# A trunk with dilated attention on one core: the odd layer in two phases, with block products for its projections

## The chip, the core and the metric

The kernel runs on one core of one Trainium2 chip. The metric is the device time of one execution in microseconds; runs are summed up by their median. TensorE (PE) multiplies matrices, with its weight loads shown apart (PEld), VectorE (DVE) and ScalarE (ACT) do element-wise work and empty PSUM, GpSimd (POOL) does element-wise work in SBUF, and SyncE (SP) issues most DMAs. Each engine works through its own instructions in order.

## What is computed

Two decoder layers on x (1024 tokens, 1024 channels), each a mixer and a gated ConvFFN, with normalisation, shift, scale and gate ahead of each. The even layer mixes by a gated delta rule and window pooling; the odd layer, which the change is about, by dilated attention in three groups, eight heads of 128 each:

```
DIL_PATTERNS = ((128, 1), (512, 4), (2048, 16))       # window, dilation
for gi, (window, dil) in enumerate(DIL_PATTERNS):
    cols = w_in[:, gi * 3 * ATT_W:(gi + 1) * 3 * ATT_W]          # 1024 x 3072
    proj = (h @ cols).reshape(B, T, 3, ATT_HEADS, ATT_DH)
    q = rms_norm(proj[:, :, 0], q_norm) * (ATT_DH ** -0.5)
    k = rms_norm(proj[:, :, 1], k_norm)
    v = proj[:, :, 2]
    o, lse = dilated_band_attention(q, k, v, dil, window // dil, slopes)
    outs.append(o); lses.append(lse)
wts = jax.nn.softmax(jnp.stack(lses), axis=0)
o = jnp.sum(wts[..., None] * jnp.stack(outs), axis=0)
return o.reshape(B, T, ATT_W) @ w_out                             # 1024 x 1024
```

The mixer's result, times a gate, is added to x; the second ConvFFN follows.

## The kernel before

Every fp32 product is three matmuls on parts: `split` (L178) rounds an operand to `hi` on ACT (L179) and subtracts it to `lo` (L180) on an engine given to it; hi·hi, hi·lo and lo·hi are summed in PSUM. Weights come as granules of 128 x 512 (`granule`, L182: a DMA on SP's queue, then a split with the engine in `lo_eng`). h, the normalised x, lies transposed in eight tiles of 128 channels x 1024 tokens, as `hh` and `hl`. There are two wide PSUM slots (`mm`, 1024 columns) and four of 512 (`sp`). `big` tiles (24) and `t2k` tiles (8) are rings of SBUF buffers.

The first FFN's up-projection (`up`, L1224) already uses seven block products: h and the weight are cut into 2 x 2 blocks, sums of blocks are formed on DVE (L1164 for h, L1219 for weights), seven products of half the size take the place of eight, and DVE adds them together (L1236).

In `odd` the projection of 9216 columns is 18 sections of 512 columns: six of v (two for each group) and twelve of queries and keys (one for each group and pair of heads, `todo`). A section is four calls of `tproj`, one for 256 tokens, of 8 k-tiles x 2 x 3 matmuls 128x512 (L1344 to L1346). A v section is copied by ACT (L1438), stored to DRAM by POOL's queue (L1441) and loaded again, gathered by the dilation (L1412). Queries and keys are normalised over each head (`qk_norm`: squares on ACT L1355, reduce on DVE L1356, `rsqrt` in small DVE operations L119 to L127, product L1362), transposed on PE (`qk_turn`, L1376) and copied to the SBUF tiles `qkT`, still in SBUF when attention reads them.

`attend` takes a pair of heads of a group in eight units (256 tokens of one head): scores (L1496), bias (DVE L1508), maximum (L1512 or L1516), its negative (L1519), exponential with its sum (ACT L1521), transposes (L1529), copy (DVE L1531 or ACT), values (L1540), copy (ACT L1542) and a DMA to DRAM (`osc`) for every group. `merge` loads the three groups' results for 128 tokens and a pair of heads, weighs them (ACT L1591, DVE L1593) and transposes the result (`turn_o`, L1599).

The order: `weave` runs a chain (here `chains`, attention and merges) and between its steps takes from `dense` (projections, then output projection) at least as much PE time as the step's `need` names: 1.7, 2.0, 1.3 or 2.4 us. Attention of a pair runs beside the projections of the next two pairs. The output projection (`update`, L216; `wide=True` uses an `mm` slot and L239) takes rows 0 to 3 while attention still runs; the four last row blocks are the edge (`edge_start`, L402), which also starts the next norm. x is stored to DRAM at the layer's start (`spill`, L1286) and loaded again for the output projection. `lo_eng` is DVE in this layer (L1287).

Of the kernel before, what the change touches and what calls it, by code (L numbers as in the profile page):

```python
# [17 lines left out]
P = 128  # L18
# [7 lines left out]
HA = 8  # L26
# [8 lines left out]
def trunk(ctx, tc, x, c, ada_w, ada_b, norm_mix, norm_ffn, ev_w_in, ev_w_out, gdn_conv_w,  # L35
# [35 lines left out]
    def t2k():  # L71
        return tmp("t2k", [P, HALF], 8)
# [1008 lines left out]
    def ffn(l, xt, h, vec, acc, vec_next):  # L1081
        gate = mod[l][:, 40:48]
        wu, wd = ffn_w_up[l], ffn_w_down[l]
        with tc.tile_pool(name=f"pf{l}", bufs=1) as pf:
# [193 lines left out]
            acc = edge(*last, v, h2)  # L1278
            return xt, h2, v, acc


    def odd(xt, h, vec, acc):
# [3 lines left out]
        spill(xs[1], xt)  # L1286
        lo_eng[0] = nc.vector  # L1287
        with tc.tile_pool(name="po", bufs=1) as po:
            def et(tag, bufs, shape=(P, HALF), dt=F32):
                return tmp(tag, shape, bufs, dt, pl=po)  # L1290
# [33 lines left out]
            def section(g, kind, i):  # L1324

                base, out_ = g * 3072, []
                for k in range(KT):
                    rows = w[k * P:(k + 1) * P, :]
                    if kind == "v":
                        out_.append(granule(rows[:, base + 2048 + i * HALF:base + 2048 + (i + 1) * HALF]))  # L1330
                    else:
                        out_.append(granule(rows[:, base:base + 2048].rearrange("p (s c) -> p s c", s=2)
                                            [:, :, i * 256:(i + 1) * 256], ("p (s c) -> p s c", dict(s=2))))
                return out_

            def tproj(wg, b2):

                ps = mm_ps()
                for k in range(KT):
                    for i in range(2):  # L1340
                        hh, hl = (t[:, (b2 * 2 + i) * P:(b2 * 2 + i + 1) * P] for t in h[k])
                        wh, wl = wg[k]
                        p = ps[:, HS[i]]
                        nc.tensor.matmul(p, hh, wh, start=(k == 0), stop=False)  # L1344
                        nc.tensor.matmul(p, hh, wl, start=False, stop=False)  # L1345
                        nc.tensor.matmul(p, hl, wh, start=False, stop=(k == KT - 1))  # L1346
                        yield 3 * MM
                return ps

            def qk_norm(ps):  # L1350

                r, rr, ra = (et(t, 2, (P, 8)) for t in ("r", "rr", "ra"))
                for i in range(2):
                    sq = t2k()
                    nc.scalar.activation(sq, ps[:, HS[i]], AF.Square)  # L1355
                    nc.vector.tensor_reduce(out=r[:, i * 4:(i + 1) * 4], in_=sq.rearrange("p (a d) -> p a d", d=P),  # L1356
                                            axis=mybir.AxisListType.X, op=ALU.add)
                rsqrt(rr, r, 1.0 / P, ra)
                qk = []
                for i in range(2):  # L1360
                    qk.append(t2k())
                    nc.vector.tensor_tensor(out=qk[i].rearrange("p (a d) -> p a d", d=P),  # L1362
                                            in0=ps[:, HS[i]].rearrange("p (a d) -> p a d", d=P),
                                            in1=rr[:, i * 4:(i + 1) * 4, None].to_broadcast([P, 4, P]), op=ALU.mult)
                return qk

            def qk_turn(i, b2, qk):

                g = todo[i][0]
                if b2 == 0:  # L1370
                    qks[i] = [et("qkT", 4, (P, 2, T)) for _ in range(2)]
                for s in range(2):
                    ps = s_ps()
                    for hh in range(2):
                        for j in range(2):
                            nc.tensor.transpose(ps[:, (hh * 2 + j) * P:(hh * 2 + j + 1) * P],  # L1376
                                                blk4(qk[j])[s * 2 + hh], ident)
                    if g == 0:
                        dst = qks[i][s][:, :, b2 * 256:(b2 + 1) * 256]
                        src = ps.rearrange("p (h f) -> p h f", h=2)  # L1380
                    else:
                        r = 4 * g
                        n = 256 // r
                        dst = qks[i][s].rearrange("p h (r l) -> p h r l", r=r)[:, :, :, b2 * n:(b2 + 1) * n]
                        src = ps.rearrange("p (h l r) -> p h r l", h=2, r=r)
                    if s == 0:
                        nc.scalar.activation(dst, src, AF.Copy, scale=gq)
                    else:
                        nc.vector.tensor_copy(dst, src)
                ready.add((i, b2))  # L1390

            todo = [(g, hp) for hq in range(2) for g in (1, 2, 0) for hp in (2 * hq, 2 * hq + 1)]
            vd = {}
            turn = []

            def run_turn(at):
                turn[0][0] -= at
                if turn[0][0] <= 0:
                    qk_turn(*turn.pop(0)[1:])

            def load_values(i):

                g, hp = todo[i]
                d = vd[(g, hp // 2)][:, hp % 2 * 256:(hp % 2 + 1) * 256]
# [12 lines left out]
            def dense():  # L1417
                for i, (g, hp) in enumerate(todo):
                    while i >= 2 and ("att", i - 2) not in ready:
                        yield None  # L1420
                    hq = hp // 2
                    if (g, hq) not in vd:
                        wg = section(g, "v", hq)
                        for b2 in range(4):
                            gen = tproj(wg, b2)
                            if i == 0 and b2 == 0:
                                weave(norm(xt, vec, h, 1, acc, (1.8, 4.5)), gen)
                            while True:
                                try:
                                    c = next(gen)  # L1430
                                except StopIteration as e:
                                    ps = e.value
                                    break
                                if turn:
                                    run_turn(1)
                                yield c
                            v = big(F32, "v")
                            nc.scalar.copy(v, ps)  # L1438
                            if b2 == 0:
                                vd[(g, hq)] = dram.tile([T, HALF], F32, name=f"vd{g}{hq}")  # L1440
                            nc.gpsimd.dma_start(vd[(g, hq)][b2 * 256:(b2 + 1) * 256].rearrange("(i p) c -> p i c", p=P),  # L1441
                                                v.rearrange("p (i c) -> p i c", i=2))
                    load_values(i)
                    wg = section(g, "qk", hp)
                    for b2 in range(4):
                        gen = tproj(wg, b2)
                        while True:
                            try:
                                c = next(gen)
                            except StopIteration as e:  # L1450
                                ps = e.value
                                break
                            if turn:
                                run_turn(1)
                            yield c
                        turn.append([10, i, b2, qk_norm(ps)])
                lo_eng[0] = nc.gpsimd
# [3 lines left out]
                for ks in ((0, 1), (2, 3)):  # L1461
                    upd = update(row_blocks(od_w_out[0], ks), o, gate, res["x"], BY_TILE, wide=True)
                    for n, c in enumerate(upd):
                        if turn:
                            run_turn(1)
                        if n == 4 and ks[0] == 0:
                            o = [from_dram(osp2[i]) for i in (2, 3)]
                        yield c
# [7 lines left out]
            def attend(i, need):  # L1476
                g, hp = todo[i]
                dil = DILS[g]
                vs = vss[i]
                vb = lambda blk, hh: vs[blk // 4][:, blk % 4 * 256 + hh * P:blk % 4 * 256 + (hh + 1) * P]  # L1480
                un = [(b2, hh) for b2 in range(4) for hh in range(2)]
                stg, sbs, spans, pTs = {}, {}, {}, {}

                def scores(n):
                    b2, hh = un[n]
                    if hh == 0:
                        stg[b2] = et("stg", 2, (P, 2, 2, 130))
# [234 lines left out]
```

## Time and profile before

| | |
|---|---|
| three runs | 3086.98, 3090.63, 3090.97 us; median 3090.63 |
| the profiled execution | 3091.38 us, of which the span (first to last instruction) 3089.7 |
| mean granted TensorE clock | 0.987 |
| odd layer: first projection matmul, first edge matmul | 1267.7 us, 2345.6 us from the span's start |
| idle PE from 1380 to 2270 us | 6.0 of 890 us |
| busy DVE and POOL from 1380 to 2270 us | 466.8 and 40.1 us |

The profile's rows name line, engine and operation, the output tile, an arrow and the inputs, then shapes, the count, busy time, and the mean of one in ns; behind the last bar stands the engine's idle time ahead of them and what ended it. In a timeline a row is start, duration, engine, and what the engine waited for. Matmuls overlap, so that their spacing, not their duration, is what one costs.

### The profile page before, as it was taken

The page shows a single profiled execution, that of the slowest core. Times are in us where ns is not written, and L with a number is a line of the kernel's source. Part 1 is how long each engine was busy: PE and PEld are TensorE (multiplying, and loading weights), DVE is VectorE, ACT ScalarE, POOL GpSimd, SP SyncE. Part 2 cuts the span into 40 slices and gives each one's busy share as a digit, 9 for nine tenths or more (in the row PEclk, how much of TensorE's full clock was granted, in tenths as well). Part 3 has the DMA queues.
Part 4 walks back from the last instruction along what each step waited for, and adds up shares of the span by engine and source line. Part 5 has one row for each costly group of instructions (what it writes and reads, how often), then busy time and mean ns, then how long its engine had stood idle before and what let it go on. Part 6 is the DMA issues. An engine that isn't in the chain of part 4 may idle for free.

```text
span 3089.7 us, 40200 instructions
## 1 busy us (share of the span) xinstructions
PE 2975.0 (96%) x14346; PEld 2444.9 (79%) x14346; DVE 2018.4 (65%) x3877; ACT 1074.4 (35%) x2170; POOL 974.9 (32%) x727
## 2 busy tenths in 40 slices
PE   6999999899999899999999999999999899999999
PEld 4777777678888777788888878888877788888888
DVE  7768745987777787754454646354687876666554
ACT  4434422433333211323333433324343433333220
POOL 4412323565555543100000010000022655555540
PEclk8999999999999999999999999999999999999999
DMA  7523323243322754231313242313243222224321
GB/s 249 143 59 102 95 83 129 72 150 109 109 86 92 248 164 123 96 96 61 106 57 113 63 154 68 115 39 118 68 164 112 85 89 82 82 82 163 113 89 59
DMA packets 275010, 331.46 MB, mean 107 GB/s; under 512 B 27411, under 2 KB 194426, under 8 KB 274810
## 3 DMA queue, kind: packets, MB, share of 16 engines
q1 hardware_dynamic: 266810, 300.55, 30.8%
q0 software_dynamic: 7040, 25.17, 2.4%
q10 hardware_dynamic: 960, 3.18, 0.3%
q8 instruction: 113, 1.85, 0.2%
q14 instruction: 87, 0.71, 0.1%
HBM read 251.82 MB, written 77.00 MB: 106 GB/s over the span
## 4 chain that ended last, share of the span: by engine, by line
PE 72%; DVE 8%; DMA 2%; issue 2%; POOL 1%; ACT 1%; SPq 0%; POOLq 0%; DVEq 0%; ACTq 0%
PE sp L202 11%; PE sp L203 11%; PE sp L204 11%; PE mm L1346 8%; PE mm L1344 8%; PE mm L1345 8%; PE mm L202 3%; PE mm L203 3%; PE mm L204 3%; PE sp L1540 2%; PE sp L1496 2%; PE sp L1376 1%; PE sp L1529 1%; DVE ada_acc L272 1%; DVE xr L1164 1%
## 5 line engine op out<-in xcount | busy, mean ns | idle before, releaser
L1344 PE MATMUL mm<-whi,hh 128*128 128x512 f32 x1152 | 482.8, 419 | 0.0
L1346 PE MATMUL mm<-whi,hl 128*128 128x512 f32 x1152 | 452.7, 393 | 0.0
L1345 PE MATMUL mm<-wlo,hh 128*128 128x512 f32 x1152 | 452.0, 393 | 0.0
L180 POOL TENSOR_TENSOR wlo<-raw,whi 128x512 fp32r<-128x512 f32 x190 | 256.1, 1363 | 552.9 <-ACT whi L179 479.1
L179 ACT ACTIVATE whi<-raw 128x512 fp32r<-128x512 f32 x334 | 207.9, 630 | 396.7 <-PE sp L203 166.4
L236 DVE SCALAR_TENSOR_TENSOR xr<-sp,mod,xr 128x512 f32<-128x512 f32 x336 | 248.2, 747 | 139.3 <-PE sp L204 138.9
L202 PE MATMUL sp<-oh,whi 128*128 128x512 f32 (+1 forms) x832 | 316.1, 380 | 18.6 <-DVE xr L236 13.1
L203 PE MATMUL sp<-ol,whi 128*128 128x512 f32 (+1 forms) x832 | 312.1, 375 | 0.0
L204 PE MATMUL sp<-oh,wlo 128*128 128x512 f32 (+1 forms) x832 | 312.0, 375 | 0.0
L202 PE MATMUL mm<-hh,whi 128*128 128x512 f32 x736 | 299.4, 407 | 9.4 <-DVE ft L1090 6.8
L203 PE MATMUL mm<-hl,whi 128*128 128x512 f32 x736 | 294.2, 400 | 3.3 <-POOL hl L373 1.6
L204 PE MATMUL mm<-hh,wlo 128*128 128x512 f32 x736 | 293.1, 398 | 0.0
L180 POOL TENSOR_TENSOR wlo<-t2k,whi 128x512 fp32r<-128x512 f32 x160 | 229.2, 1446 | 159.8 <-ACT whi L179 98.6
L1441 POOL DMA_DIRECT2D vd<-v x24 | 17.7, 736 | 771.8 <-ACT v L1438 379.6
L1346 PEld LDWEIGHTS mm<-whi,hl 128*128 128x128 f32 x1152 | 216.7, 188 | 47.9
L1345 PEld LDWEIGHTS mm<-wlo,hh 128*128 128x128 f32 x1152 | 218.0, 189 | 37.2 <-DVE wlo L180 0.2
L1344 PEld LDWEIGHTS mm<-whi,hh 128*128 128x128 f32 x1152 | 217.7, 189 | 36.4
L180 POOL TENSOR_TENSOR wlo<-wr,whi 128x512 fp32r<-128x512 f32 x114 | 179.8, 1579 | 163.4 <-ACT whi L179 161.9
L202 PEld LDWEIGHTS sp<-oh,whi 128*128 128x128 f32 x832 | 157.3, 189 | 53.0 <-DVE xr L236 18.4
L204 PEld LDWEIGHTS sp<-oh,wlo 128*128 128x128 f32 x832 | 157.3, 189 | 28.9
L203 PEld LDWEIGHTS sp<-ol,whi 128*128 128x128 f32 x832 | 157.3, 189 | 27.4
L202 PEld LDWEIGHTS mm<-hh,whi 128*128 128x128 f32 x736 | 140.4, 191 | 39.7 <-issue 10.3
(395 smaller groups left out, 6148.7 us busy)
## 6 DMA issues: line engine op xcount, KB each, us to landing
raw<-in_ada_w_dram SPq DMA_DIRECT2D x160, 256.0 KB
wr<-in_ffn_w_up_dram SPq DMA_DIRECT2D x76, 512.0 KB
raw<-in_od_w_in_dram SPq DMA_DIRECT2D x144, 256.0 KB
hid<-ft SPq DMA_DIRECT2D x44, 512.0 KB
raw<-in_ffn_w_down_dram SPq DMA_DIRECT2D x88, 256.0 KB
big<-hid SPq DMA_DIRECT2D x44, 512.0 KB
xr<-xs SPq DMA_DIRECT2D x32, 512.0 KB
os<-stg SPq DMA_DIRECT2D x96, 130.0 KB
```

Source lines behind the costliest of these rows:

```text
L179: nc.scalar.activation(dst_hi, src, AF.Copy)
L180: eng.tensor_tensor(out=dst_lo, in0=src, in1=dst_hi, op=ALU.subtract)
L202: nc.tensor.matmul(ps, wh, mh, start=first, stop=False)
L203: nc.tensor.matmul(ps, wh, ml, start=False, stop=False)
L204: nc.tensor.matmul(ps, wl, mh, start=False, stop=last)
L236: nc.vector.scalar_tensor_tensor(out=xt[o][:, s], in0=p, scalar=gate[:, o:o + 1], in1=xt[o][:, s], op0=ALU.mult, op1=ALU.add)
L272: nc.vector.scalar_tensor_tensor(out=acc, in0=raw, scalar=cs[:, k:k + 1], in1=acc, op0=ALU.mult, op1=ALU.add)
L1344: nc.tensor.matmul(p, hh, wh, start=(k == 0), stop=False)
L1345: nc.tensor.matmul(p, hh, wl, start=False, stop=False)
L1346: nc.tensor.matmul(p, hl, wh, start=False, stop=(k == KT - 1))
L1496: nc.tensor.matmul(ps[:, at:at + len(ks) * P], qks[i][0][:, hh, blk * P:(blk + 1) * P], qks[i][1][:, hh, ks[0] * P:(blk + 1) * P], start=T ...
L1540: nc.tensor.matmul(ps[:, j * P:(j + 1) * P], pTs[n][:, a0 + c * P:a0 + (c + 1) * P], vb(kb, hh), start=(c == 0), stop=(c == len(ks) - 1))
```

## The change

The odd layer's work is put in another order and most of its projections in another form.

**First phase** (`projections`). The section v(1, 0) is made by `tproj`. Then come 15 jobs, twelve of queries and keys and three of v, each 1024 x 1024 by 1024 x 512 in seven block products. A product is four token blocks x four k-tiles x three matmuls 128x256 into one `mm` slot (L1486 to L1488). While product n runs, `prep(n + 3)` forms the weight sums on DVE (L1425) and splits (ACT, and now POOL as `lo_eng`). A product's result is added to others on DVE (`plus`, L1550), or copied by ACT; one addition a job is POOL's. `finished` squares into PSUM, reduces (L1520), takes the inverse root for two quarters at a time and multiplies in place (L1510). `turn` transposes a quarter some products later and stores it to DRAM (`qkd`), 512 KB each on SP's queue, in pieces of 2 KB for group 0, 512 B for group 1 and 256 B for group 2. The v stores go to SP's queue too.

**Second phase** (`attention`). 96 units in the order of `todo`, now pair of heads by pair of heads with groups 1, 2, 0. Queries and keys come back by two DMAs of 1 MB for a set (`load_set`, issued at the third unit of the set before), v as before on POOL's queue. A unit's transposes and values come two units after its scores (before: one). Group 0's result stays in SBUF and is merged 256 tokens at a time, 16 merges where there were 32 loads of 128 tokens. Each step's need is 0.5 us. `dense` now holds v(2, 1) and v(0, 1) by `tproj`, and the output projection of rows (0, 1), (2, 3), (4, 5), each pair after the merges of its heads; the edge is left with rows 6 and 7.

The store of x is moved into the first FFN's last step: `edge(..., xs[1])` stores half tiles as they are done, 16 DMAs of 256 KB in place of eight of 512 KB.

```diff
-            acc = edge(*last, v, h2)
+            acc = edge(*last, v, h2, xs[1])
...
-        spill(xs[1], xt)
-        lo_eng[0] = nc.vector
+        lo_eng[0] = nc.gpsimd
+        todo = [(g, hp) for hp in range(HA // 2) for g in (1, 2, 0)]
+        plain = [(2, 1), (0, 1)]
+        jobs = [("qk", g, hp) for g, hp in todo] + [("v", 2, 0), ("v", 0, 0), ("v", 1, 1)]
...
+                def product(n):
+                    ps = mm_ps()
+                    wo, tb = ops.pop(n), t[TB[OPS[n % 7]]]
+                    for b in range(4):
+                        p = ps[:, b * 256:(b + 1) * 256]
+                        for k in range(KH):
+                            (wh, wl), (th, tl) = wo[k], (a[:, b * P:(b + 1) * P] for a in tb[k])
+                            nc.tensor.matmul(p, th, wh, start=(k == 0), stop=False)
+                            nc.tensor.matmul(p, th, wl, start=False, stop=False)
+                            nc.tensor.matmul(p, tl, wh, start=False, stop=(k == KH - 1))
+                        tick()
+                    return ps
...
+                for n in range(end):
+                    j, i = divmod(n, 7)
+                    prep(n + 3)
+                    ps = product(n)
+                    if i == 0:
+                        u = big(F32, "u")
+                        nc.scalar.copy(u, ps)
+                    elif i == 1:
+                        g0 = acc_t()
+                        plus(g0, u, ps)
+                        finished(j, 0, 0, g0)
+                    elif i == 2:
+                        plus(u, u, ps)
+                    elif i == 3:
+                        v, g1 = acc_t(), acc_t()
+                        nc.scalar.copy(v, ps)
+                        plus(g1, u, ps)
+                    elif i == 4:
+                        plus(u, u, ps)
+                        plus(v, v, u, nc.gpsimd)
+                        finished(j, 1, 1, v)
+                    elif i == 5:
+                        plus(g1, g1, ps)
+                        finished(j, 0, 1, g1)
+                    else:
+                        plus(u, u, ps)
+                        finished(j, 1, 0, u)
...
+                upd = update(row_blocks(od_w_out[0], (0, 1)), o, gate, res["x"], BY_TILE, wide=True)
+                yield from upd
+                while ("m", 1) not in ready:
+                    yield None
...
-                acc2, tl, n = edge_start(row_blocks(od_w_out[0], (4, 5, 6, 7)), res["m2"] + res["m3"], gate, res["x"], xs[3])
+                acc2, tl, n = edge_start(row_blocks(od_w_out[0], (6, 7)), res["m3"], gate, res["x"], xs[3])
...
+                    if n < UN:
+                        i = n // 8
+                        if n % 8 == 2 and i + 1 < len(todo):
...
+                            load_set(i + 1)
                         scores(n)
                         yield need
-                    if n:
-                        turn_p(n - 1)
+                    if 0 <= n - 2 < UN:
+                        turn_p(n - 2)
                         yield need
-                        values(n - 1)
-                        yield need
+                        values(n - 2)
+                        if ot is not None:
+                            load_others(*ot)
+                        yield need
```

What this does to PE's order in the projections. Before, in the middle of the layer (`mm` is a section's PSUM tile, `hh` and `hl` a tile of h, `whi` and `wlo` a weight granule):

```order
L1344 MATMUL mm_13713<-whi_13508,hh_10378 128x512
L1345 MATMUL mm_13713<-wlo_13509,hh_10378 128x512
L1346 MATMUL mm_13713<-whi_13508,hl_10379 128x512
L1496 MATMUL sp_13747<-qkT_13148,qkT_13147 128x128 x2
L1344 MATMUL mm_13713<-whi_13514,hh_10380 128x512
L1345 MATMUL mm_13713<-wlo_13515,hh_10380 128x512
L1346 MATMUL mm_13713<-whi_13514,hl_10381 128x512
```

Scores of the pair before (L1496) stand between two chunks. The same engine in the first phase of the changed kernel; the operand named `qkT` here is a sum of blocks of h that borrows such a tile:

```order
L1486 MATMUL mm_12086<-whi_11857,qkT_11091 128x256
L1487 MATMUL mm_12086<-wlo_11858,qkT_11091 128x256
L1488 MATMUL mm_12086<-whi_11857,qkT_11091 128x256
L1486 MATMUL mm_12086<-whi_11861,qkT_11094 128x256
L1487 MATMUL mm_12086<-wlo_11862,qkT_11094 128x256
L1488 MATMUL mm_12086<-whi_11861,qkT_11094 128x256
```

The matmuls are half as wide, and no attention stands among them. On DVE, in the same phase, the last two additions of a job (L1550, `mm` being the product) with what stands between them: the end of the inverse root (L125 to L127), the multiplication by it (L1510) and the reduces of the next quarter (L1520):

```order
L1550 TENSOR_TENSOR acc_15387<-acc_15387,mm_15487 128x1024
L125 SCALAR_TENSOR_TENSOR ra_15456<-rr_15455,r_15232 128x16
L126 TENSOR_TENSOR ra_15456<-ra_15456,rr_15455 128x16
L127 SCALAR_TENSOR_TENSOR rr_15455<-ra_15456,rr_15455 128x16
L1510 TENSOR_TENSOR acc_15230<-acc_15230,rr_15455 128x1024
L1510 TENSOR_TENSOR acc_15386<-acc_15386,rr_15455 128x1024
L1520 TENSOR_REDUCE r_15537<-sp_15538 128x4
L1520 TENSOR_REDUCE r_15537<-sp_15541 128x4
L1550 TENSOR_TENSOR u_15167<-u_15167,mm_15558 128x1024
```

The next addition, which empties the next product's PSUM slot, stands behind the whole of that. Last, PE beside attention. Before, a unit's values (L1540) and transposes (L1529) stand among projection matmuls:

```order
L1540 MATMUL sp_16689<-v_15451,sb_16610 128x128 x3
L1344 MATMUL mm_16754<-whi_16708,hh_10372 128x512
L1345 MATMUL mm_16754<-wlo_16709,hh_10372 128x512
L1346 MATMUL mm_16754<-whi_16708,hl_10373 128x512
L1344 MATMUL mm_16754<-whi_16714,hh_10374 128x512
L1345 MATMUL mm_16754<-wlo_16715,hh_10374 128x512
L1346 MATMUL mm_16754<-whi_16714,hl_10375 128x512
L1344 MATMUL mm_16754<-whi_16714,hh_10374 128x512
L1529 MATMUL sp_16694<-ident,sb_16676 128x128
```

Now, in a stretch of the second phase without dense work (L1699 scores, L1732 transposes, L1744 values, L1787 the transposes of a merged result):

```order
L1744 MATMUL sp_22032<-v_21597,t2k_21945 128x128
L1744 MATMUL sp_22032<-v_21598,t2k_21945 128x128 x3
L1787 MATMUL sp_22038<-ident,t2k_21928 128x128 x4
L1699 MATMUL sp_22052<-qkT_21834,qkT_21833 128x128
L1699 MATMUL sp_22052<-qkT_21834,qkT_21833 128x256
L1732 MATMUL sp_22064<-ident,t2k_21968 128x128 x4
L1744 MATMUL sp_22070<-v_21598,t2k_21969 128x128 x4
L1699 MATMUL sp_22103<-qkT_21834,qkT_21833 128x128
```

Only attention's own matmuls follow one another there. Elsewhere in the phase chunks of the two v sections or of the output projection stand between them as before.

More of the change, by code (lines that the diff above doesn't have):

```diff
@@ L1322, in tok_rows, with v_granule, tproj @@
                 return d.rearrange("(l r) h e -> r l h e", r=8)[blk]
[L1324 to L1336, printed above, removed]
+            def v_granule(g, hq, k):
+                c0 = g * 3072 + 2048 + hq * HALF
+                return granule(w[k * P:(k + 1) * P, c0:c0 + HALF])
+            def tproj(wg, b2, between=None):
                 ps = mm_ps()
@@ L1347, in tproj @@
                         yield 3 * MM
-                return ps
[L1350 to L1365, printed above, removed]
@@ L1392, in odd, with v_out @@
[L1392 to L1401, printed above, removed]
+                    if between is not None:
+                        between(k)
+                return ps
+            def v_out(g, hq, b2, ps, v):
+                nc.scalar.copy(v, ps)
+                nc.sync.dma_start(vd[g, hq][b2 * 256:(b2 + 1) * 256].rearrange("(i p) c -> p i c", p=P),
+                                  v.rearrange("p (i c) -> p i c", i=2))
@@ L1417, in dense @@
             def dense():
[L1418 to L1444, printed above, removed]
-                    for b2 in range(4):
[L1446 to L1456, printed above, removed]
@@ L1457, in dense, with more @@
-                lo_eng[0] = nc.gpsimd
+                wg = wg0
+                for n, (g, hq) in enumerate(plain):
+                    nxt = []
+                    def more(k):
+                        if n + 1 < len(plain):
+                            nxt.append(v_granule(*plain[n + 1], k))
+                    for b2 in range(4):
+                        ps = yield from tproj(wg, b2, more if b2 == 3 else None)
+                        v_out(g, hq, b2, ps, big(F32, "v"))
+                    ready.add(("vd", g, hq))
+                    wg = nxt
@@ L1544, in values @@
+                    nc.scalar.copy(stg[i, b2][:, :, hh, 0:P], ps[:, :256].rearrange("p (a f) -> p a f", a=2))
+                    if hh and g:
                         for j in range(2):
                             rows = tok_rows(osc[g], g, b2 * 2 + j)
-                            nc.sync.dma_start(rows[:, hp * 2:hp * 2 + 2, :], stg[b2][:, j])
-                for n in range(9):
-                    if n < 8:
-                        key = (i, un[n][0] if g == 0 else 3)
-                        yield lambda: key in ready
+                            nc.sync.dma_start(rows[:, hp * 2:hp * 2 + 2, :], stg[i, b2][:, j])
@@ L1622, in chains @@
-            def chains():
-                last = len(todo) - 1
-                for i in range(last):
-                    yield lambda: (i, 0) in ready
-                    yield from attend(i, 1.7)
-                    if i == 5:
-                        yield from merge(0, 2.0)
-                        yield from merge(1, 2.0)
-                other = merge(2, 0)
-                for n, need in enumerate(attend(last, 1.3)):
-                    yield need
-                    if n % 2:
-                        next(other, None)
-                drain(other)
-                yield from merge(3, 2.4)
@@ L1638, in odd, with chain @@
-            dn = dense()
-            weave(chains(), dn)
-            drain(dn)
-            lo_eng[0] = nc.gpsimd
+                    if to is not None:
+                        turn_o(*to)
+                        yield need / 2
+            with tc.tile_pool(name="pob", bufs=1) as pb_:
+                load_set(0)
+                def chain():
+                    yield 10.0
+                    yield from attention(pb_, 0.5)
+                dn = dense()
+                weave(chain(), dn)
+                drain(dn)
```

389 lines of the change are left out of this document (286 added, 103 removed).

## The prediction

> **What bounds the kernel now.** I read the page first (engines, then the chain that ended last), then the windows of the odd layer, then single lines.
>
> ```profile
> span 3089.7 us, 40200 instructions
> PE 2975.0 (96%) x14346; PEld 2444.9 (79%) x14346; DVE 2018.4 (65%) x3877; ACT 1074.4 (35%) x2170; POOL 974.9 (32%) x727
> ...
> PE 72%; DVE 8%; DMA 2%; issue 2%; POOL 1%; ACT 1%; SPq 0%; POOLq 0%; DVEq 0%; ACTq 0%
> ```
>
> PE is busy 96% of the span and makes up 72% of the chain. That average hides stages, so here are windows of the odd layer. Columns: busy us of PE, PEld, DVE, ACT, POOL, then the granted clock and the DMA share. The last row is a stretch of the first FFN's up-projection.
>
> ```profile
> 1267.40:1380.00 112.60, 109.73 (x502) 89.69 (x502) 66.37 (x154) 36.86 (x56) 19.62 (x24) 1.00 0.35 115
> 1380.00:2270.00 890.00, 884.05 (x4527) 739.12 (x4526) 466.78 (x1402) 323.01 (x839) 40.13 (x50) 1.00 0.27 86
> 2270.00:2345.00 75.00, 66.22 (x320) 53.94 (x319) 65.94 (x182) 32.84 (x94) 21.91 (x15) 0.95 0.60 196
> 2345.00:2412.00 67.00, 61.28 (x272) 48.96 (x271) 47.28 (x88) 23.64 (x41) 21.89 (x14) 0.97 0.31 106
> 2460.00:2520.00 60.00, 60.00 (x264) 49.08 (x263) 44.48 (x51) 23.68 (x36) 37.26 (x26) 1.00 0.37 114
> ```
>
> For 890 us PE idles 6 us: the odd layer is a row of matmuls, with the attention of the pair before slipped between them. From 2270 to 2345 the last attention and the merges are left over; there DVE is busy 65.94 of 75.00 us (88%) and PE waits. So a matmul removed ahead of 2270 is worth its time only if attention's vector work stays covered.
>
> **Part 1: fifteen sections become block products.** First the price of a matmul, from starts in an unbroken run, at 512 columns and at 256.
>
> ```profile
> 1299.67 0.39 PE L1345 MATMUL mm<-wlo,hh 128*128 128x512 f32 x1
> ...
> 1303.98 0.39 PE L1346 MATMUL mm<-whi,hl 128*128 128x512 f32 x1
> ```
>
> ```profile
> 3033.66 0.28 PE L202 MATMUL sp<-oh,whi 128*128 128x256 f32 x1
> ...
> 3035.89 0.28 PE L203 MATMUL sp<-ol,whi 128*128 128x256 f32 x1
> ```
>
> Each fence spans 19 steps: 4.31/19 = 0.2268 us and 2.23/19 = 0.1174 us. A section was 4 x 8 x 2 x 3 = 192 of the first kind, 43.55 us. A job is 7 products x 4 x 4 x 3 = 336 of the second, 39.45 us. That saves 4.10 us, and 61.5 us for 15 jobs.
>
> What a job asks of DVE, which before spread over the whole layer: 6 additions of 1024 columns (priced by L239), 8 weight sums (the mean of L1219's four groups, 0.943), 8 reduces (L1356), 24 small operations (L126, taken as 0.2), 4 multiplications of 1024 columns (L1090).
>
> ```profile
> L239 DVE SCALAR_TENSOR_TENSOR xr<-mm,mod,xr 128x1024 f32<-128x1024 f32 x32 | 41.0, 1280 | 17.9 <-PE mm L204 17.9
> L1219 DVE TENSOR_TENSOR t2k<-wr,wr 128x512 f32<-128x512 f32 x38 | 49.8, 1309 | 0.0
> L1219 DVE TENSOR_TENSOR t2k<-wr 128x512 f32<-128x512 f32 x38 | 39.6, 1041 | 6.8 <-DMA wr<-in_ffn_w_up_dram 6.8
> L1219 DVE TENSOR_TENSOR t2k<-t2k,wr 128x512 f32<-128x512 f32 x38 | 28.2, 741 | 2.8
> L1219 DVE TENSOR_TENSOR t2k<-wr,t2k 128x512 f32<-128x512 f32 x38 | 25.8, 679 | 0.0
> L1356 DVE TENSOR_REDUCE r<-t2k 128x4 f32<-128x512 f32 x96 | 62.4, 682 | 100.1 <-ACT t2k L1355 99.8
> L126 DVE TENSOR_TENSOR ra<-ra,rr 128x8 f32<-128x8 f32 x144 | 24.6, 171 | 4.4
> L1090 DVE SCALAR_TENSOR_TENSOR ft<-ft,cols,ft 128x1023 f32<-128x1023 f32 x80 | 118.9, 1487 | 5.5 <-ACT ft L1094 5.3
> L180 POOL TENSOR_TENSOR wlo<-t2k,whi 128x512 fp32r<-128x512 f32 x160 | 229.2, 1446 | 159.8 <-ACT whi L179 98.6 <-PE sp L204 53.8 <-DVE ada_acc L272 3.5
> L180 POOL TENSOR_TENSOR ol<-big,oh 128x1024 fp32r<-128x1024 f32 x50 | 124.4, 2491 | 131.8 <-ACT oh L179 66.6 <-PE sp L203 57.6 <-PE sp L204 3.4
> ```
>
> DVE: 7.7 + 7.5 + 5.5 + 4.8 + 5.9 = 31.4 us. POOL: 14 x 1.446 + 2.49 = 22.7 us. PE needs 39.45 us and, in a query and key job, 32 transposes; eight of these take 0.87 us by the next two rows, so 3.48 us, as before.
>
> ```profile
> 1375.32 1.03 PE L1376 MATMUL sp<-ident,t2k 128*128 128x128 f32 x8
> 1376.19 0.39 PE L1496 MATMUL sp<-qkT,qkT 128*128 128x128 f32 x2
> ```
>
> So PE is the longest at 42.9 us, and the additions beside it are covered. The order within DVE matters: between the last two additions of a job stand three small operations, two multiplications and two reduces, 5.0 us, with the addition 6.3 us against the 5.6 us of a product; two PSUM slots give 11.2 us, so PE need not wait. The first FFN runs this same scheme with no idle PE (60.00 of 60.00 above). I allow 10 us in all for starts and late operands (the opening window above idles 2.9 us), between 0 and the lock priced below.
>
> The moved DMAs: SP takes the stores of v from POOL's queue and gains 48 stores of 512 KB of queries and keys, later 24 loads of 1 MB. On POOL nothing now waits behind the v stores, but it gains the subtractions that DVE did before. On SP a store waits for its ACT copy, and the next job's weight loads stand behind it; each is due three products (17 us) later, which covers such a wait.
>
> ```profile
> q1 hardware_dynamic: 266810, 300.55, 30.8%
> ```
>
> That is 0.308 x 3089.7 x 16 / 266810 = 57 ns of one DMA engine for a packet. The smallest pieces (256 B, group 2) make 8192 packets in a job: 8192 x 0.057 / 16 = 29 us, inside a job of 43 us. Hidden at 0; without cover up to 4 x 29 us, but only if all else filled the engines, whose share in the odd layer is 0.27 to 0.35.
>
> **Part 2: attention with what is left.** DVE's rows for one unit (a head, 256 tokens), and a merge:
>
> ```profile
> L1508 DVE SCALAR_TENSOR_TENSOR sb<-bm,sp 128x384 f32<-128x384 f32 (+1 forms) x64 | 38.5, 601 | 86.7 <-PE sp L1496 86.6
> L1508 DVE SCALAR_TENSOR_TENSOR sb<-bd,sp 128x256 f32<-128x256 f32 x32 | 13.4, 419 | 58.3 <-PE sp L1496 58.3
> L1512 DVE TENSOR_REDUCE stg<-sb 128x2 f32<-128x256 f32 (+1 forms) x56 | 29.9, 534 | 1.7
> L1516 DVE TENSOR_REDUCE stg<-sb 128x1 f32<-128x128 f32 x80 | 24.8, 347 | 1.4
> L1519 DVE TENSOR_SCALAR neg<-stg 128x2 f32<-128x2 f32 x96 | 17.2, 179 | 2.6
> L1531 DVE COPY sb<-sp 128x384 f32<-128x384 f32 (+2 forms) x48 | 26.1, 543 | 55.0 <-PE sp L1529 55.0
> L1593 DVE SCALAR_TENSOR_TENSOR t2k<-ld,me,t2k 128x128 f32<-128x128 f32 x128 | 44.0, 397 | 3.0 <-ACT t2k L1591 2.8
> ```
>
> The first six sum to 149.9 us for 96 units: 1.56 us each. A merge of 256 tokens is now 8 x 0.344 (44.0/128) and six small ones near 0.18: 3.85 us. For PE, this row is one of three alike lines in the 890 us window:
>
> ```profile
> 1380.00:2270.00 890.00, 425.09 (x1007) 190.27 (x1006) 1.00 0.27 86
> ```
>
> 3 x 1007 x 0.2268 = 685 us, 6 idle; the other 199 us hold 43 of the 48 octets and a half of transposes (some 41 us with those of the merges) and about 90 units: 1.75 us of PE each.
>
> The order of PE in the changed kernel gives the sharing. Units 0 to 39 get 408 dense matmuls: 92.5 + 70 = 162.5 us, PE the longer. Three later stretches, 22 units, get 222: 50.3 + 38.5 = 89 us, with DVE near 76. The other 34 units are all but bare: 42 dense matmuls, because each pair of output rows waits for its head pair's merge. There DVE has 34 x 1.56 = 53, made 58 as half of them are group 0 with its longer rows, 8.5 merges 33, splits and evacuations 8: 99 us. At the 88% busy of the window 2270 to 2345, 99/0.88 = 112 us; PE's own 69 us hides under it. Bounds: 99 (DVE packed full) and the clock rival's 152. Together 363.4 us.
>
> **The sum**, on the profiled run (3091.4 us, with 1.7 outside the span; the median of the runs shown is 3090.6). Its places:
>
> ```profile
> L1438 ACT COPY v<-mm x24: 989/1014/1016, 1293.2 to 2153.7; 128x1024 f32<-128x1024 f32 x24
> 2345.55 0.47 PE L202 MATMUL sp<-oh,whi 128*128 128x512 f32 x1
> ```
>
> The first v pass ends at 1293.2 and is kept. Then 3 passes 32.7, 15 jobs 591.7, transposes 12 x 3.48 = 41.8, waits 10, hand-over to the first attention 2, second phase 363.4, and 7 from the last unit to the edge (a merge of 3.9, splits and transposes; bounds 2 and 12): 2341.8. Before, the edge starts at 2345.55: only 3.7 us gained, since the 61.5 us are nearly all given back as DVE-bound time. The edge itself loses 96 matmuls, 21.8 us, less 4 us for operands that come later in proportion (it idled 5.7 us before; bounds 0 and 10): -17.8. Sum -21.5, so 3069 us by the median. The edge that stores x as it goes costs nothing: the same bytes as the 8 stores of 512 KB, under the FFN's last matmuls; uncovered, a few us.
>
> **The rivals.** *Everything packs.* DVE runs full in the bare stretches (-13), no late operands (-10), hand-over, tail and edge tight (-11): 34 us less, 3035 us. For it: lookahead of two units instead of one. Against: the 2270 window, where DVE had 12% left over and PE still waited.
>
> *The clock drops* (the slower side). Rows of PE after an idle of 2 us:
>
> ```profile
> 2399.74 0.39 PE L202 MATMUL mm<-hh,whi 128*128 128x512 f32 x1
> 2402.14 0.66 PE L303 MATMUL sp<-ident,t2k 128*128 128x128 f32 x4 [2.02 <-DVE t2k L343]
> 2402.87 0.58 PE L204 MATMUL mm<-hh,wlo 128*128 128x512 f32 x1
> 2403.25 0.63 PE L202 MATMUL sp<-hh,whi 128*128 128x512 f32 x1
> 2403.68 0.63 PE L203 MATMUL sp<-hl,whi 128*128 128x512 f32 x1
> ```
>
> After it a matmul starts 0.43 us after the last, not 0.23. If PE idles a third of the time in the bare stretches and stays at that half clock, its 34 x 1.75 + 42 x 0.2268 = 69 us become 138; it then joins DVE in the chain of each unit, and at 0.9 busy the stretches take 152: +40, 3109 us. It decides from 134 us on, where the gain is used up. Against: the 2270 window was granted 0.95 in the mean, at 88% busy. [...]
>
> *No gain: phase 1 locks.* The same weight sum takes 1309 or 679 ns by its operands (L1219 above), so two SBUF inputs beside a busy POOL may be slower than I took; POOL now has 22.7 us a job. At the dearest group 8 sums cost 8 x (1.309 - 0.943) = 2.9 us more; passed on to PE whole in every job that is 44 us, 3113, the upper bound. I take half, 22 us: 3091. [...] Against this rival: the FFN window above, where POOL is busy 37.26 and DVE 44.48 of 60 and PE idles nowhere.
>
> **How the numbers follow.** About 0.2%, 6.2 us, is what a measurement of this kernel can tell from no change. Forecast 0.45 (own range 3055 to 3084), packed 0.18, clock 0.20, lock 0.17, of which 0.13 ends within 6.2 us and 0.04 above. Faster 0.45 + 0.18 = 0.63, same 0.13, slower 0.24. The range reaches from the packed case to the upper bound of the lock, 3035 to 3113.
>
> **What would show it.** Right: products of 5.6 us without idle PE in phase 1; first attention matmul near 1971; edge near 2342, with DVE about 88% busy and PE idle in the stretches without dense work; edge some 18 us shorter. Wrong: PE waiting on additions or weight splits in phase 1 (lock); a granted clock under 0.8 in the second phase (clock); DVE above 95% there (packed); or the second phase waiting on DMAs, which I hold hidden: the loads of a set's queries and keys, or the return of groups 1 and 2 before a merge.

## The result and the profile after

The changed kernel takes 3197.5 us (median of 4 runs, 3193.8 to 3202.6) against 3089.4 us of the kernel before (median of 4, 3087.0 to 3091.0): a ratio of 1.035, 95% interval 1.034 to 1.036. The forecast was 3069 us, faster, with a range that ended at 3113. It is 108 us slower.

The page of the changed kernel, its span, its engines and its chain:

```profile
span 3193.4 us, 44933 instructions
PE 2968.8 (93%) x16506; PEld 2543.7 (80%) x16506; DVE 2118.9 (66%) x3495; ACT 1176.2 (37%) x2330; POOL 1343.6 (42%) x964
...
PE 62%; DVE 11%; POOL 5%; issue 3%; DMA 3%; ACT 2%; SPq 0%; POOLq 0%; DVEq 0%; ACTq 0%
```

PE's share of the chain fell from 72% to 62%, and POOL, hardly on it before, has 5%. The windows say where: a stretch of query and key jobs, a stretch of v jobs, and three stretches of the second phase without dense work (columns as before: PE, PEld, DVE, ACT, POOL, granted clock, DMA share):

```profile
1500.00:1600.00 100.00, 91.41 (x740) 91.06 (x740) 63.81 (x100) 39.35 (x65) 43.54 (x30) 0.95 0.31 84
2000.00:2050.00 50.00, 50.00 (x419) 50.00 (x419) 12.84 (x11) 15.12 (x24) 34.28 (x28) 1.00 0.39 116
2255.00:2293.50 38.50, 23.63 (x145) 19.99 (x144) 23.95 (x71) 19.16 (x63) 5.30 (x5) 0.87 0.50 168
2341.00:2382.00 41.00, 24.71 (x140) 20.37 (x139) 25.16 (x83) 19.45 (x69) 3.82 (x5) 0.83 0.57 187
2429.00:2467.00 38.00, 25.35 (x147) 20.99 (x145) 26.60 (x86) 21.85 (x76) 2.51 (x2) 0.91 0.27 78
```

The v jobs run as forecast: PE busy 50 of 50, at a granted clock of 1.00. The query and key jobs lose 8.6% of PE and 5% of its clock, and DVE is busy only 64% there. In the bare stretches neither PE nor DVE is busy for more than 70%: something is waited for in turn. What PE waits for, from 1290 to 2450 us (total, times, longest):

```profile
PE sp L1532 <- DVE acc L1510: 51.6, 12, 4.4
PE sp L1744 <- DVE t2k L1734: 33.6, 17, 7.5
PE sp L1744 <- ACT t2k L1736: 13.1, 17, 3.8
```

The first is a wait of 4.3 us in each of the 12 query and key jobs, ahead of the transposes of `turn` (L1532). The chain of waits through one of them, in order of time:

```profile
1461.91 2.56 POOL wlo L180 x2
1464.47 2.81 POOL acc L1550
...
1467.31 0.61 ACT sp L1519
...
1467.94 1.30 DVE r L1520 x2
...
1469.27 1.19 DVE r L119
...
1470.47 1.23 DVE rr L121
...
1473.16 1.13 DVE acc L1550
...
1474.83 1.24 DVE acc L1510
1476.06 0.14 issue
1476.20 1.94 PE sp L1532 x8
```

Product 4 of a job gives a quarter that POOL adds (behind two weight splits), ACT squares, DVE reduces, takes the inverse root of and multiplies. The transposes stand seven blocks, 10 us, behind that product in PE's order; the chain takes 14. All later products stand behind the transposes, though their operands have long been ready. And when PE goes on, it goes on at half speed:

```profile
1471.63 0.28 PE L1488 MATMUL mm<-whi,t 128*128 128x256 f32 x1
1476.20 1.94 PE L1532 MATMUL sp<-ident,acc 128*128 128x128 f32 x8 [4.29 <-DVE acc L1510]
1477.79 0.56 PE L1486 MATMUL mm<-whi,t 128*128 128x256 f32 x1
...
1481.78 0.41 PE L1486 MATMUL mm<-whi,hh 128*128 128x256 f32 x1
1481.99 0.32 PE L1487 MATMUL mm<-wlo,hh 128*128 128x256 f32 x1
```

Eight transposes take 1.59 us (0.79 without the wait ahead), and matmuls start 0.21 us apart until 1482, where before the wait it was 0.12. The places of the sum: attention's first scores, and the first and last starts of a matmul of the edge.

```profile
L1699 PE MATMUL sp<-qkT,qkT x384: 270/275/634, 2068.0 to 2454.4; 128*128 128x128 f32 x104, 128*128 128x256 f32 x88
L202 PE MATMUL sp<-qkT,whi x32: 389/389/774, 2467.4 to 2495.5; 128*128 128x512 f32 x32
```

The first scores come 97 us later than forecast (2068.0 against 1971.4). Of these, 11 us are 48 matmuls of v(2, 1), which stand between the last product and the first scores (the second phase's first step asks for 10 us of dense work) and which the forecast counted in the second phase:

```profile
2056.95 0.28 PE L1488 MATMUL mm<-whi,t 128*128 128x256 f32 x1
2057.07 0.40 PE L1352 MATMUL mm<-whi,hh 128*128 128x512 f32 x1
...
2067.75 0.39 PE L1354 MATMUL mm<-whi,hl 128*128 128x512 f32 x1
```

From the first scores the second phase takes 399.4 us against 370.4 with its tail, and the edge 28 us between its first and last start, where it took 50.

### The profile page after: what moved, and what is told of

The parts are those of the page before. It is cut to its first block, busy times and chain, and to the rows that moved or that the text cites. A ratio compares the mean times of both kernels' runs of the same rounds, so it can differ in the third digit from the quotient of the medians.

```text
span 3193.4 us, 44933 instructions
## 1 busy us (share of the span) xinstructions
PE 2968.8 (93%) x16506; PEld 2543.7 (80%) x16506; DVE 2118.9 (66%) x3495; ACT 1176.2 (37%) x2330; POOL 1343.6 (42%) x964
## 4 chain that ended last, share of the span: by engine, by line
PE 62%; DVE 11%; POOL 5%; issue 3%; DMA 3%; ACT 2%; SPq 0%; POOLq 0%; DVEq 0%; ACTq 0%
PE sp L202 10%; PE sp L203 10%; PE sp L204 10%; PE mm L1486 4%; PE mm L1487 4%; PE mm L1488 4%; PE mm L203 3%; PE mm L204 3%; PE mm L202 3%; POOL wlo L180 3%; PE sp L1744 2%; PE sp L1532 2%; PE sp L1699 1%; POOL acc L1550 1%; PE mm L1354 1%
## 5 line engine op out<-in xcount | busy, mean ns | idle before, releaser
L180 POOL TENSOR_TENSOR wlo<-raw,whi 128x512 fp32r<-128x512 f32 x334 | 455.9, 1376 | 824.9 <-ACT whi L179 608.9
L180 POOL TENSOR_TENSOR wlo<-t2k,whi 128x512 fp32r<-128x512 f32 x250 | 350.3, 1411 | 387.0 <-ACT whi L179 238.9
L1486 PE MATMUL mm<-whi,hh 128*128 128x256 f32 x960 | 276.5, 288 | 4.6 <-ACT acc L1361 3.0
L1487 PE MATMUL mm<-wlo,hh 128*128 128x256 f32 x960 | 273.8, 285 | 0.0
L1488 PE MATMUL mm<-whi,hl 128*128 128x256 f32 x960 | 273.4, 285 | 0.0
L180 POOL TENSOR_TENSOR wlo<-wr,whi 128x512 fp32r<-128x512 f32 x114 | 179.3, 1575 | 167.7 <-ACT whi L179 164.5
L179 ACT ACTIVATE whi<-t2k 128x512 fp32r<-128x512 f32 x250 | 155.9, 628 | 227.5 <-PE mm L203 86.9
L1486 PEld LDWEIGHTS mm<-whi,hh 128*128 128x128 f32 x960 | 187.2, 195 | 5.0 <-ACT acc L1361 3.2
L180 POOL TENSOR_TENSOR ol<-big,oh 128x1024 fp32r<-128x1024 f32 x50 | 123.3, 2467 | 161.4 <-ACT oh L179 99.1
L1487 PEld LDWEIGHTS mm<-wlo,hh 128*128 128x128 f32 x960 | 187.0, 195 | 0.0
L1488 PEld LDWEIGHTS mm<-whi,hl 128*128 128x128 f32 x960 | 186.4, 194 | 0.0
```

Source lines behind the costliest of these rows:

```text
L179: nc.scalar.activation(dst_hi, src, AF.Copy)
L180: eng.tensor_tensor(out=dst_lo, in0=src, in1=dst_hi, op=ALU.subtract)
L1486: nc.tensor.matmul(p, th, wh, start=(k == 0), stop=False)
L1487: nc.tensor.matmul(p, th, wl, start=False, stop=False)
L1488: nc.tensor.matmul(p, tl, wh, start=False, stop=(k == KH - 1))
```

## The experiments

The theory after the result has two parts. In phase 1, PE's own in-order queue is the bound: the transposes reach it ahead of their operand, and after the idle time PE runs at about half rate for a while (0.21 us a matmul in place of 0.12). In phase 2, the units without dense work are bound by PE's turns with the copies, not by DVE's throughput. The main rival: DVE and POOL hold each other up, and a job simply needs 50 us of them. Ratios are to the kernel before, run on the same chip.

**Transposes later.** The first pair's transposes stand one product later:

```diff
-                        turns.append([7 if n == 0 else 3, (g, i), c_, th_, q_])
+                        turns.append([(11 if th else 7) if n == 0 else 3, (g, i), c_, th_, q_])
```

> The change with one edit: the transposes of a job's first two finished quarters stand four blocks (one product) later on PE. Theory (PE's own queue: in each of the 12 query and key jobs the transposes reach PE 4.3 us before DVE has multiplied their operand, and after that idle the clock is halved for some 6 us, about 3.6 us more): the 51.6 us of that wait go, the granted clock between 1400 and 1900 us goes from 0.93-0.95 to 1.00, a job takes 43 to 44 us instead of 50.9, and the time is 3197 - 95 = about 3102. Rival 1 (DVE and POOL hold each other up, so a job needs about 50 us of them): the wait only moves to another place, over 3175. Rival 2 (the clock is low because of the half-wide matmuls themselves): the idle goes, the clock stays at 0.93-0.95, about 3145.

Measured: 3136.9 us, ratio 1.015 (1.013 to 1.018), 61 us less. The window of the jobs and the largest wait of PE in phase 1:

```profile
1500.00:1600.00 100.00, 96.58 (x804) 95.65 (x804) 75.46 (x118) 41.19 (x71) 49.84 (x33) 1.00 0.34 90
```

```profile
PE mm L1486 <- DVE ra L125: 13.2, 12, 1.2
```

The wait is gone, the clock is 1.00 in this window, DVE gets more done in the same 100 us: it was not the bound, and both rivals fall. The size was too high. The first scores start at 2005.2, 62.8 us earlier, but 5.0 of that is an earlier start of the whole layer (its first projection matmul at 1263.12 us against 1268.15), so the edit took 58 us from phase 1. PE's listed waits in the phase fall from 56 to 18 us, 38 of it (a new one of 1.1 us a job appears); the other 20 us are the clock, less some small new delays. Counted in the trace of the change, the clock cost about 25 us, 2.1 a job: after a wait, 8 transposes and 5 to 20 matmuls ran at half rate. I had expected a job to go from 50.9 to 43 or 44 us; it goes from 50.4 to 45.4, because the clock cost 2.1 us and not the 3.6 that I took, and the new wait came in.

**Transposes earlier**, the other way and for both pairs of a job (3 in place of 7):

```diff
-                        turns.append([7 if n == 0 else 3, (g, i), c_, th_, q_])
+                        turns.append([3 if n == 0 else 3, (g, i), c_, th_, q_])
```

> The change with one edit, the other way round: the transposes of both finished pairs of a job stand four blocks (4 x 12 x 0.12 = 5.8 us of PE work) earlier. Theory (PE's queue waits for an operand whose time is set by the chain through ACT, POOL and DVE): the wait of the first pair grows from 4.3 to about 10 us, and the second pair starts to wait; per job at least 5.8 us more, so 3197 + 12 x 5.8 = 3267 or more, up to 3340 if the second pair waits 5.8 us as well. Rival (DVE and POOL work sets a job's length, wherever the transposes stand): within 10 us of 3197.

One run: 3271.8 us, 74 us above the change, at the size of the theory. The split is another: the two pairs wait about alike (24 waits, 4.3 us in the mean; the two shares of them in windows that meet at 1990), instead of 10 us and little.

```profile
PE sp L1532 <- DVE acc L1510: 94.8, 22, 5.4
...
PE sp L1532 <- DVE acc L1510: 9.2, 2, 5.4
```

The rival, for which the place does not count, is out.

**POOL's addition on DVE.**

```diff
-                        plus(v, v, u, nc.gpsimd)
+                        plus(v, v, u)
```

> The change with one edit: the one addition of a job that POOL made (2.86 us in the profile, and behind POOL's weight splits) is made by DVE. It stands in the chain that the transposes wait for. Theory (PE's own queue waits for that chain): the chain is 1.5 to 3 us shorter, the wait of 4.3 us a job falls to 1.3 to 2.8, and with a shorter idle the clock may stay up: 20 to 70 us less, 3127 to 3177. Rival 1 (DVE and POOL hold each other up, DVE being the bound): DVE gets 1.2 to 2.4 us a job more, the time is 0 to 30 us longer, 3197 to 3227.

Measured: 3196.1 us, ratio 1.034 (1.032 to 1.035): no change, a miss. The wait is 4.1 us instead of 4.3. DVE's timeline shows why:

```profile
1465.78 1.21 DVE L1550 TENSOR_TENSOR acc<-acc,u 128x1024 f32<-128x1024 f32 x1
...
1471.75 1.22 DVE L1550 TENSOR_TENSOR acc<-acc,mm 128x1024 f32<-128x1024 f32 x1
...
1473.80 0.69 DVE L1520 TENSOR_REDUCE r<-sp 128x4 f32<-128x512 f32 x1
...
1474.48 0.69 DVE L1520 TENSOR_REDUCE r<-sp 128x4 f32<-128x512 f32 x1
...
1476.34 2.36 DVE L1510 TENSOR_TENSOR acc<-acc,rr 128x1024 f32<-128x1024 f32 x2
```

The quarter is added sooner, but beside the addition that stood there before (L1550 with `mm`) the reduces of the next quarter now stand between its reduce and its multiplication. A link shortened ahead of an in-order queue was filled with other work of that queue.

**Scores between transposes and values**, phase 2 alone:

```diff
-                        scores(n)
-                        yield need
-                    if 0 <= n - 2 < UN:
-                        turn_p(n - 2)
-                        yield need
+                    if 0 <= n - 2 < UN:
+                        turn_p(n - 2)
+                        yield need
+                    if n < UN:
...
+                        scores(n)
+                        yield need
+                    if 0 <= n - 2 < UN:
                         values(n - 2)
```

> The change with one edit in the second phase: the scores of unit n are issued between the transposes and the values of unit n - 2, not ahead of both. Theory (where no dense work is left, PE stands behind the copy of the transposed probabilities, 52 us of waits in all, because nothing lies between a unit's transposes and its values): the copy of 0.5 to 0.7 us is covered by scores of 0.7 us, the 34 bare units take 2.8 to 3.2 us in place of 4.3, and the time is 20 to 45 us less, 3152 to 3177. Rival (the stretches wait for DVE's work, or for the DMAs of the merges): under 8 us less, or none.

Measured: 3177.7 us, ratio 1.027 (1.026 to 1.029), 20 us less, at the lower end. Waits of values for both copies fall from 52 to 27 us, and a wait of 14 us for the exponential (L1724) comes up. The second phase takes 384.4 us in place of 399.4. The order counts, but most of the bare stretches' length stays.

**Both edits.**

> The edits of the later transposes in the first phase and of the scores between transposes and values in the second, together. If both causes are as held and lie in separate phases, the gains add up: 95 + 20 to 45, so 3057 to 3082, below the kernel before (3089). If phase 1 is bound by DVE and POOL, or phase 2 by DVE and DMAs, it stays above 3100.

Measured: 3122.2 us, ratio 1.010 (1.008 to 1.011): 75 us less than the change. The two gains add up (61 + 20 would be 81), so the causes lie in separate phases. The 3057 to 3082 expected is missed because both gains were smaller than I held, and the kernel stays slower than before.

**A third plain section as cover**, with both edits: v(1, 1) leaves phase 1 and lies beside attention as 192 matmuls.

```diff
-        plain = [(2, 1), (0, 1)]
-        jobs = [("qk", g, hp) for g, hp in todo] + [("v", 2, 0), ("v", 0, 0), ("v", 1, 1)]
+        plain = [(1, 1), (2, 1), (0, 1)]
+        jobs = [("qk", g, hp) for g, hp in todo] + [("v", 2, 0), ("v", 0, 0)]
```

> Both edits of the run before (later transposes, scores between) and one more: the section v(1, 1) is no longer a block-product job of phase 1 but a third section of 192 matmuls 128x512 beside attention. By the order of PE the dense matmuls then last to unit 87 instead of leaving 34 units bare. Theory (the second phase lost its time in units without dense work): phase 1 is 40 us shorter, phase 2 needs 864 x 0.2268 + 96 x 1.75 = 364 us of PE, and about 15 for its ends, so about 380 where it took 385; 3122 - 45 = about 3077, below the kernel before. Rival (phase 2 is bound by DVE, DMA or the merges, and not by missing cover): phase 2 grows by the 43.5 us, 3120 to 3128.

Measured: 3089.7 us (median of 10), ratio 0.999 (0.998 to 1.001): as fast as the kernel before, 33 us less than both edits alone. In the profiled execution, the longest of the ten (3099.5 us), phase 1 is 37 us shorter (scores from 1975.5 instead of 2012.8). Phase 2 got 43.5 us of PE work and grew by 10 us, from 385 to 395: most of it went into time that had been idle. That is 15 us more than the theory's 380, and the time misses the 3077 expected by 13. One place of this is a pair's first merge, in DVE's and then PE's timeline:

```profile
2046.80 0.17 DVE L1765 TENSOR_REDUCE mx<-ld 128x4 f32<-128x12 f32 x1 [5.46 <-DMA ld<-os]
```

```profile
2049.47 2.07 PE L1744 MATMUL sp<-v,t2k 128*128 128x128 f32 x8 [4.20 <-ACT t2k L1736]
```

DVE stands behind the load of the other groups' results, ACT behind DVE, and the values behind ACT's copy.

**The same with the old order of scores.** The order of the change, with the third section and the later transposes:

> As the run with three plain sections, but with scores, transposes and values in the order of the change. If PE waits for the copy only where nothing else stands between, dense chunks now stand there in nearly all units, and the edit of the order is worth under 8 us: 3077 to 3085. If the order counts by itself, it is 15 to 20 us slower than the other, as it was without the third section.

Measured: 3095.9 us, ratio 1.001 (1.000 to 1.002), 6 us above (second phase 401.8 us against 395.2): with dense work between, the order is worth about a third of what it was without. So the copies cost most where nothing else stands between. The 3077 to 3085 expected is missed with the run that it builds on.

**The same with POOL's addition on DVE.**

> As the run with three plain sections, with POOL's addition made by DVE. Alone on the change that edit did nothing, because other work of DVE filled the gap ahead of the multiplication. With the transposes out of the way, what is left of PE's waits in phase 1 is 12 times 1.1 us for an addition of DVE that stands behind the reduces of the quarter that POOL adds. Theory: those waits shrink, 5 to 13 us less than the run with three plain sections. Rival: DVE's extra 1.2 to 2.4 us a job takes the gain back, within 4 us of it.

Measured: 3094.5 us, ratio 1.001 (1.000 to 1.002), 5 us above the run with three plain sections. The waits of 13.2 us go, and others of 16.9 us for the additions (L1550) come, and phase 1 is 4 us longer; the rival was nearer.

**Fewer chunks at the merges**, `yield need / 2` after a merged result's transposes replaced by `yield 0`:

> As the run with three plain sections, but the chain no longer asks for a dense chunk after the transposes of a merged result: 16 x 3 matmuls are left for later units, and by the order of PE the last bare units are 5 instead of 7. Theory (bare units at the end cost 3 to 5 us, units with nine dense matmuls 3.2 to 3.7): 3 to 10 us less than that run, 3080 to 3087 against about 3090. Rival (the end is bound by DVE's merges): no change, within 3 us.

Measured: 3093.6 us, ratio 1.001 (1.000 to 1.001): no gain. The last eight units, up to the edge, took 36.8 us with 12 dense matmuls where they took 35.9 with none: a dense chunk more or less there does not move the end. That DVE's merges are the reason, as the rival has it, is not shown.

**And merges one unit later:**

```diff
-                    ot, mg, to = group0(n - 2, 0), group0(n - 4, 1), group0(n - 6, 1)
+                    ot, mg, to = group0(n - 2, 0), group0(n - 5, 1), group0(n - 7, 1)
```

> As the run with the spread chunks, and each merge and the transposes of its result one unit later. In the run with three plain sections DVE waits 5.5 us for the load of the other groups' results at a pair's first merge, and PE stands 4.2 us behind it (units 20, 44). Theory (the merge is issued too soon behind its load): 2 to 4 us less at each of four pairs, 8 to 15 us less, 3070 to 3080. Rival (there are only two buffers for a merge, and later merges hold back the group 0 units that need the third): 0 to 15 us longer.

Measured: 3100.0 us, ratio 1.003 (1.002 to 1.004), 6 us slower than the run before it. The theory is out: DVE's waits for the merges' loads hardly change (26.6 us against 28.2), and the last eight units take 43.2 us in place of 36.8. The time is what the rival expected, but its cause, the two buffers, is not shown; a run with a third `ld` buffer, which would tell, is missing.

## Why the prediction was wrong

**Failed: "So PE is the longest at 42.9 us, and the additions beside it are covered."** Throughput was summed rightly: DVE has 64% and POOL 44% of the time in phase 1, and PE is the longest. But I checked only one thing that PE waits for, the PSUM slots. The transposes stand in PE's queue too, a fixed number of blocks behind the product, and their operand comes through ACT, POOL and DVE one after another. That chain of 14 us against 10 us of cover cost 51.6 us of idle PE. It was to be had beforehand: seven blocks stand in the code, and most links had a price in the prediction.

**Failed in its place: the clock rival.** PE does run slower after idle time here (0.21 us a matmul after the waits of 4.3 us, 0.12 before them), but I looked for it in phase 2 alone. In phase 1 it took 25 us. In phase 2 the granted clock was 0.94 in the mean and 0.83 to 0.91 in the bare windows, not under the 0.8 that the rival named.

**Mis-sized: a matmul at 256 columns.** 0.1200 us in the products against the 0.1174 of the last output projection (why they differ is open); here is the unbroken run, 20 steps in 2.40 us:

```profile
2019.99 0.28 PE L1486 MATMUL mm<-whi,hh 128*128 128x256 f32 x1
...
2022.39 0.28 PE L1488 MATMUL mm<-whi,hl 128*128 128x256 f32 x1
```

With 5040 of them that is 13 us. The gain of a job is 43.55 - 40.3 = 3.2 us, not 4.1, and 49 us in all instead of 61.5. With 51.6 for the waits, 25 for the clock and the 11 of v(2, 1) that only stand on the other side of the first scores, it makes 101 us for the 97 by which the first scores came late; the forecast had allowed 12 us for other waits and the hand-over, and not all of it was needed.

**Failed: "At the 88% busy of the window 2270 to 2345."** The bare stretches, tail included, took 145 us in place of 112 + 7. DVE is busy for 61 to 70% of the windows shown. What fits is a turn of transposes, copy, values and next scores on PE, with merges between that wait for their loads; the new order (15 us off phase 2) and the added cover (43.5 us of work for 10 us) bear this out in part, and how the rest divides between copies and loads stays open. The loads are a sign of being wrong that the prediction had named, the return of groups 1 and 2 before a merge:

```profile
DVE mx L1765 <- DMA ld<-os: 17.6, 10, 3.9
```

The window I took 88% from had output projection matmuls beside attention, so it was no model of a bare one. The dense stretches came out near. Units 0 to 39 took 155 us; the forecast's 162.5 becomes 151.6 without the 48 matmuls that ran before them. The three later stretches took 99 us (89 forecast); what is over lies in unit 56 with 21.6 us, where the output projection's operand is late (ACT splits it only when its load has landed) and PE then runs at half rate, a matmul each 0.43 us:

```profile
2298.25 1.06 ACT L179 ACTIVATE oh<-big 128x1024 fp32r<-128x1024 f32 x1 [4.20 <-DMA big<-osp]
```

```profile
2299.36 1.22 PE L202 MATMUL mm<-oh,whi 128*128 128x512 f32 x2 [5.27 <-ACT oh L179]
...
2308.52 0.63 PE L202 MATMUL mm<-oh,whi 128*128 128x512 f32 x1
2308.95 0.63 PE L203 MATMUL mm<-ol,whi 128*128 128x512 f32 x1
```

**Held:** the hidden DMAs of phase 1 (none of PE's listed waits there, 56 us, ended with a DMA), the free store of x (the first v pass ends at 1293.8, 0.6 us later), and the edge: 22 us less between its first and last start, and 18 us less from its first start to the end of the span, against 17.8. That phase 2 gives the gain of the block products back held in sign alone: phase 1 had no gain to give (a job took 50.4 us, a section with its transposes 47.0), and phase 2 is not bound by DVE.

**The lock rival** (no gain, 3091) named the wrong price. DVE was held up beside POOL here (small operations took 1.2 us in place of 0.17, as the next but one section shows), and two such delays of 1 us lie in the chain that PE waits for. But when the transposes moved, the same work of both fitted into 45.4 us a job. So these delays lengthen the chain; they do not bound the phase.

## What to carry to other kernels

A sum of busy times finds the bound only if nothing in the bounding engine's own queue waits. So go through each instruction kind of that queue, and for each compare the work that stands between it and its operand's first producer with the sum of the links between them. And take cover away only where the work left is itself a pipeline that fills an engine: here 43.5 us of extra matmuls beside attention lengthened it by 10 us.

## What the runs showed of the hardware

Small DVE operations took 1.2 us instead of 0.17 where POOL was subtracting. DVE, then POOL, in the changed kernel:

```profile
1469.27 1.18 DVE L119 TENSOR_SCALAR r<-r 128x16 f32<-128x16 f32 x1
1470.47 1.22 DVE L121 TENSOR_SCALAR rr<-r 128x16 int32<-128x16 int32 x1
1471.73 0.17 DVE L123 TENSOR_SCALAR rr<-rr 128x16 int32<-128x16 int32 x1
```

```profile
1469.12 1.29 POOL L180 TENSOR_TENSOR wlo<-raw,whi 128x512 fp32r<-128x512 f32 x1 [1.85 <-ACT whi L179]
1470.37 1.30 POOL L180 TENSOR_TENSOR wlo<-t2k,whi 128x512 fp32r<-128x512 f32 x1
```

The first ends at 1470.45 and the second at 1471.69, within 0.04 us of POOL's two ends (1470.41 and 1471.67); the third, with POOL idle, takes 0.17. In the whole trace 40 of the 516 operations of the inverse root (L119 to L127) took over 1 us, and each of the 40 started while POOL was at work on a subtraction (L180) and ended within 0.04 us of that subtraction's end; of the 473 under 0.3 us only one started while POOL was at work.

PE ran at about half its rate (a matmul of 256 columns each 0.21 us in place of 0.12) after each of the 12 idle times of 4.3 us, for 2.8 to 5.9 us, and in unit 56 (512 columns, each 0.43 us in place of 0.23) after 5.27 us for some 12 us, with two more waits of 1.21 us in them. In the kernel before it did so after 2.02 us of idle, for about 4 us (0.43 us a matmul, the prediction's rows from 2399.74). In the run with later transposes it kept a granted clock of 1.00 from 1400 to 2000 us, with idle times of up to 1.2 us. How long an idle time must be for PE to slow down, and what ends the slow stretch, these runs do not settle.
